# Per-token factors turned once and broadcast from DRAM, and the queries' factor moved into the exponential

## The chip, the cores and the metric

The kernel runs on one core of one Trainium2 chip. Its time is the device time of one execution in microseconds (us). The core has TensorE (PE; its weight loads are listed apart as PEld), VectorE (DVE), ScalarE (ACT), GpSimd (POOL), and SyncE (SP), which in this kernel issues every DMA, in order. TensorE writes its results to PSUM, eight banks of 128 partitions x 512 float32; the other tiles lie in SBUF.

## The reference

One decoder layer on 1024 tokens of width 1024, in float32. Each norm multiplies a token by a factor of its own, and the change is about those factors and about the one of the mLSTM heads:

```python
def rmsnorm(x, g):
    y = xf * lax.rsqrt(jnp.mean(xf * xf, axis=-1, keepdims=True) + EPS)
    return (y * g).astype(x.dtype)

h = rmsnorm(x, ln1[l]);  z = h @ w_in[l]
...                                    # 4 mLSTM heads (dh 128), 8 forgetting-attention heads (dh 64)
mh = mlstm_chunkwise(mq, mk, mv, ig, lf)
mh = mh * lax.rsqrt(jnp.mean(mh * mh, axis=-1, keepdims=True) + EPS)
mh = mh * ml_norm[l]
ml_out = mh * sigmoid(ml_o)
x = x + concatenate([ml_out, fx_out]) @ w_out[l]
x = x + cross_attention(rmsnorm(x, ln_x[l]), rmsnorm(mem, ln_mem[l]), w_xq[l], w_xkv[l], w_xo[l])
u = relu(rmsnorm(x, ln2[l]) @ w_ff1[l]);  x = x + (u * u) @ w_ff2[l]
return rmsnorm(x, ln_f)

def cross_attention(h, memn, w_q, w_kv, w_o):          # 4 heads of 256, 256 memory tokens
    q = h @ w_q
    ...
    s = einsum('bqhd,bmhd->bhqm', q, k) * (X_DH ** -0.5)
    p = softmax(s, axis=-1)
    ...
```

## The kernel before

**Layout and precision.** Activations lie feature-major: 128 features on the partitions, tokens along the free axis, in two halves of 512 tokens (`hf` 0 and 1). A product is made of three matmuls (`mm3`, L184 to L186) of a high and a low part of each operand; `split` (L129) cuts a tile in two: ScalarE writes the high part (L132, with a scale L135), VectorE the low part (L133, with a scale L136). A weight tile is loaded to `wr` (L172, two buffers), cut to `wh` and `wl` (three buffers each), and used for 24 matmuls of 512 columns for each half.

**A factor per token.** A norm's factor is made token-major: sums of squares by matmuls against a column of ones (L233, L216), then `rsqrt_cols` (L192), small VectorE steps around one power on GpSimd (L202), give a column tile [128 tokens, n blocks] such as `rcol` or `fac`. Feature-major data need it along the free axis, the same on all partitions. `spread` (L209) does that: for each block of 128 tokens one float32 matmul of the column, broadcast over 128 columns as weights, against the identity; the result is a PSUM bank, read from there or copied by ScalarE to the constant tile `row` [128, 1024] (`row_m` for the memory tokens).

**Where factors are spread.** (1) The first norm: half 0 inside the hand-ordered first stage (L391 to L394), half 1 in `spread_second` (L407), called between two token blocks of `token_major`. Readers: every projection of the mLSTM and the forgetting heads (L489, L618, L643). (2) The memory norm in `mem_prepare` (L283). (3) Each mLSTM head: at the end of `ml_head` (L601 to L610) the factor `fac` is spread half by half; two VectorE multiplies, a split and two stores to `mix` follow. (4) The cross-attention norm, after each half of the mixer's second projection (L1042); the readers are the queries (L1052) and `xo_sink` (L1199). (5) The final factor `inv`, at job 30 of the first MLP product (L1390 to L1394); `stretch` (L1370) then rescales the residual with it, tile by tile through DRAM. (6) `finish` (L1482), the last norm.

**The mLSTM loop.** `ml_project(hd)` (L631) makes a head's projections: keys with a convolution (`conv_silu`), the forgetting heads' queries (`fx_project(0)`), the carried state, queries, forgetting keys, output gate. `ml_head(hd)` (L551) does the head's attention: it loads the decay row `nmb` by a broadcast from the DRAM tile `rows` into the buffer "a" (L558), exponentials of it on ScalarE (L569), a mask on GpSimd (L571), the multiply with the scores on VectorE (L572). Program order is `ml_head(0)`, `ml_project(1)`, `ml_head(1)` and so on.

**Order.** Except for stages in `in_order()`, which chains the instructions of each compute engine in the order written (the first stage, and every `slot` of the forgetting attention, L938), a planner sets each engine's order and the order of SP's issues: it runs through the program with a model of the durations and takes, in program order of preference, what is ready. On the chip each engine then keeps that order. Tiles are taken by tag from rotating buffers (`BUFS`, L70: "a" and "y" one, the others two); a tile waits until the one before it in its buffer has been read or stored.

**Cross attention.** `cross_head` (L1046), one for each head and half: two products of 24 matmuls into the banks `mm` and `m2`; for each, VectorE multiplies by 1/16 and by `row` into `qf` (L1052) and `qf` is split; then scores, maximum (L1070), exponential (L1072), reciprocal, transposes (L1080), values.

## Time and profile before

Three runs took 1584.74, 1588.86 and 1590.78 us (median 1588.86). The profiled execution took 1586.37 us; its span, from the first to the last instruction, is 1584.7 us, at a mean granted TensorE clock of 0.991.

| stage | stretch (us) | TensorE busy (us) | VectorE busy (us) | DMA share |
|---|---|---|---|---|
| first norm, first values | 0 to 40 | 32.70 | 29.30 | 0.59 |
| mLSTM values, gates, first head | 40 to 180 | 137.75 | 88.93 | 0.27 |
| mLSTM heads | 180 to 330 | 150.00 | 101.36 | 0.31 |
| last head, fox values | 330 to 440 | 106.44 | 62.13 | 0.58 |
| forgetting attention | 440 to 640 | 192.62 | 145.70 | 0.73 |
| mixer's projection | 640 to 700 | 55.90 | 45.73 | 0.82 |
| cross heads | 700 to 850 | 150.00 | 80.20 | 0.38 |
| cross output, begin of MLP | 850 to 960 | 109.26 | 93.11 | 0.46 |
| first MLP product | 960 to 1200 | 232.22 | 197.24 | 0.76 |
| second MLP product | 1200 to 1540 | 338.98 | 239.22 | 0.66 |
| last norm and output | 1540 to 1585 | 28.50 | 25.08 | 0.29 |

In the profile's lines a group is named by its line in the kernel, its engine, its operation and the tiles it writes and reads ("sc<-ident,c_fac": a PSUM tile of the tag sc from the identity and the column tile fac). In the timeline the columns are start, duration, engine (SPq: SP's queue, the issue of a DMA), line, operation, tiles, and in brackets the idle time of the engine before it and what ended it. A wait is written "who waits <- for whom: us in total, times, longest".

### The profile page before, as it was taken

The page shows a single profiled execution, that of the slowest core. Times are in us where ns is not written, and L with a number is a line of the kernel's source. Part 1 is how long each engine was busy: PE and PEld are TensorE (multiplying, and loading weights), DVE is VectorE, ACT ScalarE, POOL GpSimd, SP SyncE. Part 2 cuts the span into 40 slices and gives each one's busy share as a digit, 9 for nine tenths or more (in the row PEclk, how much of TensorE's full clock was granted, in tenths as well). Part 3 has the DMA queues.
Part 4 walks back from the last instruction along what each step waited for, and adds up shares of the span by engine and source line. Part 5 has one row for each costly group of instructions (what it writes and reads, how often), then busy time and mean ns, then how long its engine had stood idle before and what let it go on. Part 6 is the DMA issues. An engine that isn't in the chain of part 4 may idle for free.

```text
span 1584.7 us, 22226 instructions
## 1 busy us (share of the span) xinstructions
PE 1534.4 (97%) x7836; PEld 1280.1 (81%) x7836; DVE 1108.0 (70%) x1752; ACT 724.1 (46%) x1323; POOL 440.3 (28%) x476
## 2 busy tenths in 40 slices
PE   8999999999999999999999999999999999999995
PEld 8888888889887887778888877777778778888885
DVE  7656666665677785765457887888877877766775
ACT  7324343333577673544344466666665422111153
POOL 0003030413344431421100022433343543333314
PEclk9999999999999999999999999999999999999998
DMA  5322222435686857853344438777877966656632
GB/s 209 112 73 91 100 87 90 126 107 162 214 238 194 262 211 263 297 198 122 120 140 154 163 123 294 243 270 272 279 259 280 380 262 239 239 239 239 253 133 107
DMA packets 123271, 310.72 MB, mean 196 GB/s; under 512 B 13764, under 2 KB 28228, under 8 KB 115224
## 3 DMA queue, kind: packets, MB, share of 16 engines
q1 hardware_dynamic: 123160, 309.31, 56.2%
q8 instruction: 61, 1.00, 0.3%
q14 instruction: 50, 0.41, 0.1%
HBM read 205.24 MB, written 104.02 MB: 195 GB/s over the span
## 4 chain that ended last, share of the span: by engine, by line
PE 46%; DVE 8%; DMA 7%; ACT 3%; issue 3%; POOL 1%; SPq 0%; DVEq 0%; ACTq 0%; POOLq 0%
PE sc L184 4%; PE sc L186 4%; PE sc L185 4%; PE tp L184 3%; PE tp L186 3%; PE tp L185 3%; PE m L184 3%; PE mm L184 3%; PE mm L186 3%; PE mm L185 3%; PE m L186 3%; PE m L185 3%; PE ov L184 2%; PE ov L185 2%; PE ov L186 2%
## 5 line engine op out<-in xcount | busy, mean ns | idle before, releaser
L132 ACT ACTIVATE wh<-wr 128x1024 fp32r<-128x1024 f32 (+2 forms) x105 | 105.4, 1005 | 136.6 <-PE mm L186 35.2
L184 PE MATMUL tp<-act,wl 128*128 128x512 f32 (+1 forms) x388 | 152.4, 393 | 1.4 <-ACT row L1287 0.7
L185 PE MATMUL tp<-act,wh 128*128 128x512 f32 (+1 forms) x388 | 151.8, 391 | 0.0
L186 PE MATMUL tp<-act,wh 128*128 128x512 f32 (+1 forms) x388 | 151.6, 391 | 0.0
L133 DVE TENSOR_TENSOR wl<-wr,wh 128x1024 fp32r<-128x1024 f32 (+2 forms) x105 | 127.2, 1213 | 21.3 <-ACT wh L132 20.9
L184 PE MATMUL m<-act,wl 128*128 128x512 f32 (+1 forms) x348 | 135.2, 389 | 1.0 <-DVE wl L133 0.6
L186 PE MATMUL m<-act,wh 128*128 128x512 f32 (+1 forms) x348 | 133.4, 383 | 0.0
L185 PE MATMUL m<-act,wh 128*128 128x512 f32 (+1 forms) x348 | 133.3, 383 | 0.0
L184 PE MATMUL mm<-act,wl 128*128 128x512 f32 (+1 forms) x308 | 119.9, 389 | 2.9 <-DVE wl L133 1.3
L185 PE MATMUL mm<-act,wh 128*128 128x512 f32 (+1 forms) x308 | 118.3, 384 | 0.0
L186 PE MATMUL mm<-act,wh 128*128 128x512 f32 (+1 forms) x308 | 118.3, 384 | 0.0
L184 PE MATMUL sc<-act,wl 128*128 128x512 f32 (+1 forms) x296 | 114.9, 389 | 2.8 <-DVE wl L133 2.2
L185 PE MATMUL sc<-act,wh 128*128 128x512 f32 (+1 forms) x296 | 114.1, 386 | 0.0
L186 PE MATMUL sc<-act,wh 128*128 128x512 f32 (+1 forms) x296 | 113.5, 385 | 0.0
L1358 POOL TENSOR_TENSOR z<-wr 128x256 f32<-128x256 f32 x56 | 50.5, 922 | 168.1 <-DMA wr<-w_ff2q 132.1
L132 ACT ACTIVATE w<-wr 128x768 fp32r<-128x768 f32 (+1 forms) x30 | 24.5, 818 | 153.7 <-PE sc L186 82.9
L184 PEld LDWEIGHTS tp<-act,wl 128*128 128x128 f32 x388 | 72.9, 188 | 18.8 <-DVE wl L133 1.5
L186 PEld LDWEIGHTS tp<-act,wh 128*128 128x128 f32 x388 | 72.9, 188 | 16.2
L185 PEld LDWEIGHTS tp<-act,wh 128*128 128x128 f32 x388 | 72.9, 188 | 15.9
L132 ACT ACTIVATE wh<-z 128x1024 fp32r<-128x1024 f32 (+1 forms) x54 | 55.5, 1028 | 59.6 <-POOL z L1358 26.9
L184 PEld LDWEIGHTS m<-act,wl 128*128 128x128 f32 x348 | 65.6, 189 | 15.1 <-DVE wl L133 1.0
L186 PEld LDWEIGHTS m<-act,wh 128*128 128x128 f32 x348 | 65.4, 188 | 13.3
(657 smaller groups left out, 4288.2 us busy)
## 6 DMA issues: line engine op xcount, KB each, us to landing
act<-right SPq DMA_DIRECT2D x49, 1024.0 KB
right<-w SPq DMA_DIRECT2D x56, 256.0 KB
wr<-w_ff2q SPq DMA_DIRECT2D x28, 512.0 KB
wr<-w_ff SPq DMA_DIRECT2D x25, 512.0 KB
right<-r_d SPq DMA_DIRECT2D x49, 256.0 KB
right<-r_e SPq DMA_DIRECT2D x49, 256.0 KB
act<-fqk SPq DMA_DIRECT2D x48, 256.0 KB
wr<-w_in SPq DMA_DIRECT2D x20, 512.0 KB
```

Source lines behind the costliest of these rows:

```text
L132: s.activation(hi, src, AF.Copy)
L133: return v.tensor_tensor(out=lo, in0=src, in1=hi.bitcast(F32), op=ALU.subtract)
L184: nc.tensor.matmul(ps, w[1], x[0], start=first, stop=False, skip_group_check=more)
L185: nc.tensor.matmul(ps, w[0], x[1], start=False, stop=False, skip_group_check=more)
L186: nc.tensor.matmul(ps, w[0], x[0], start=False, stop=last, skip_group_check=more)
L1358: g.tensor_tensor(out=o, in0=x, in1=y, op=op)
```

## The change

A new helper `to_row` turns a column tile of n blocks into n rows by one TensorE transpose, copies the small result to SBUF on ScalarE, stores it in a DRAM tile, and loads it back with a broadcast over all 128 partitions. It takes the place of `spread` in the cases (1) to (5); `finish` keeps it. Besides that:

- The first norm's two halves are laid out together, between token blocks 1 and 2 of `token_major` (`row_first`).
- In `ml_head` the part from the spread on becomes three later steps of a generator: it stops after `fac`, and `ml_project` of the next head continues it after its key projection (transpose, store, load of half 0), after `fx_project(0)` (multiplies, split, stores of half 0; load of half 1) and after `carried` (the same of half 1). For the last head the steps come after the slots 2, 6 and 10 that lead the forgetting attention in. The rows are loaded into the buffer "a"; the fox values (`fv_sink`) rotate through "b", "p", "c" in place of "b", "a", "c".
- The cross norm of half 0 is worked out after the third output tile of half 1 of the mixer's projection, that of half 1 after the first cross head.
- The queries are no longer multiplied by the norm's factor: PSUM is split at once with the scale 1/16, and the factor enters the exponential as its scale per partition (there tokens lie on the partitions, so `rcol` serves as it is); the maxima are multiplied by it.
- The final factor of both halves is laid out at job 30 at once.

```diff
+    rowd = dram.tile([4, T], F32, name="rowd")
+
+    def to_row(dst, cols, n, at, bank=None):
+
+        ps = (bank or ov_)()
+        nc.tensor.transpose(ps[:n, :P], cols, ident)
+        s.activation(dst[:n, :P], ps[:n, :P], AF.Copy)
+        load(at.rearrange("o (t q) -> (o t) q", t=n), dst[:n, :P])
+        w = min(dst.shape[1], n * P)
+        return load(dst, at[:, :w].broadcast_to([P, w]))
...
-        s.activation(row_m, rsqrt_row(acc, rcol_m, 2, 2), AF.Copy)
+        rsqrt_sums(acc, rcol_m, 2, 2)
+        to_row(row_m, rcol_m, 2, rowd[1:2, :NM])
...
-                ps = ov_()
-                spread(ps, rcol[:, 0:4], 4)
-                s.activation(row[:, 0:TH], ps, AF.Copy)
...
-    def spread_second():
-        ps = ov_()
-        spread(ps, rcol[:, 4:8], 4)
-        s.activation(row[:, TH:], ps, AF.Copy)
+    def row_first():
+        to_row(row, rcol, 8, rowd[0:1])
...
+    facd = dram.tile([MLH, T], F32, name="facd")
...
         v.tensor_tensor(out=fac, in0=fac, in1=rd, op=ALU.mult)
+        yield
         for hf in range(2):
-            fb = sc()
-            spread(fb, fac[:, 4 * hf : 4 * hf + 4], 4)
+            fb = w2("a")
+            at = facd[hd : hd + 1]
+            if hf == 0:
+                to_row(fb, fac, 8, at, sc)
+            else:
+                load(fb, at[:, TH:].broadcast_to([P, TH]))
+            yield
             y = nums[hf]
...
-        o = rotate("b", "a", "c").bitcast(F32R).rearrange("p (h e c) -> p h e c", h=4, e=2)
+        o = rotate("b", "p", "c").bitcast(F32R).rearrange("p (h e c) -> p h e c", h=4, e=2)
...
+    closing = iter(())
...
         yk = conv_silu(MLH + hd, *k)
+        next(closing, None)
         fx_project(0, hd)
+        next(closing, None)
         state = carried(hd, yk)
+        next(closing, None)
         yq = conv_silu(hd, *q)
...
-    token_major(a["w_mv"], mv_sink, (1,), {2: spread_second, 4: gate_rows})
+    token_major(a["w_mv"], mv_sink, (1,), {2: row_first, 4: gate_rows})
...
-        ml_head(hd, *ready)
+        closing = ml_head(hd, *ready)
+        next(closing)
...
-    for _ in range(LEAD_):
+    for i in range(LEAD_):
         slot(False, 0)
+        if i in (2, 6, 10):
+            next(closing, None)
...
             split(hi[:, n], lo[:, n], t, vec[:, VEC["ln_x"] + n :][:, 0:1])
             square_sum(acc, t, n == 0, add=g)
             if hf == 1 and n == KT - 3:
                 mix_done.append(done)
+            if hf and n == 2:
+                row_second(0, acc0)
+
+        def row_second(hf, acc):
+            c = rcol[:, 4 * hf : 4 * hf + 4]
+            rsqrt_sums(acc, c, 4)
+            at = slice(hf * TH, hf * TH + TH)
+            to_row(row[:, at], c, 4, rowd[2:3, at])
 
         out_proj(a["w_out_b"], mix_fx[hf], hf, full_sink)
-        s.activation(row[:, hf * TH : hf * TH + TH], rsqrt_row(acc, rcol[:, 4 * hf : 4 * hf + 4], 4), AF.Copy)
         h2.append((hi, lo))
+        acc0 = acc
...
-                qf = w2("f")
-                v.scalar_tensor_tensor(out=qf, in0=ps, scalar=1.0 / 16.0, in1=row[:, hf * TH : hf * TH + TH], op0=ALU.mult, op1=ALU.mult)
-                split(*t, qf)
+                split(*t, ps, 1.0 / 16.0)
...
                 v.tensor_reduce(out=mxc[:, i - 1 : i + 1], in_=sp, axis=mybir.AxisListType.X, op=ALU.max, negate=True)
+
+                v.tensor_tensor(out=mxc[:, i - 1 : i + 1], in0=mxc[:, i - 1 : i + 1], in1=rcol[:, 4 * hf + i - 1 : 4 * hf + i + 1], op=ALU.mult)
         for i in range(4):
-            s.activation(pr[:, i], sps[i // 2][:, i % 2], AF.Exp, bias=mxc[:, i : i + 1], accum_out=den[:, i : i + 1])
+            s.activation(pr[:, i], sps[i // 2][:, i % 2], AF.Exp, bias=mxc[:, i : i + 1], scale=rcol[:, 4 * hf + i : 4 * hf + i + 1], accum_out=den[:, i : i + 1])
...
             for _ in steps:
                 pass
+            if hd == hf == 0:
+                row_second(1, acc0)
...
-            for hf in range(2):
-                ps = bank()
-                spread(ps, inv[:, 4 * hf : 4 * hf + 4], 4)
-                s.activation(row[:, hf * TH : hf * TH + TH], ps, AF.Copy)
+            to_row(row, inv, 8, rowd[3:4], bank)
```

More of the change, by code (lines that the diff above doesn't have):

```diff
@@ L1035, in full_sink @@
                     mix_fx.append(mix_load(MLH + KX, KT, 1))
+            split(hi[:, n], lo[:, n], t, vec[:, VEC["ln_x"] + n :][:, 0:1])
+            square_sum(acc, t, n == 0, add=g)
             if hf == 1 and n == KT - 3:
                 mix_done.append(done)
-            split(hi[:, n], lo[:, n], t, vec[:, VEC["ln_x"] + n :][:, 0:1])
-            square_sum(acc, t, n == 0, add=g)
+            if hf and n == 2:
[5 more added lines that the diff above has]
+            to_row(row[:, at], c, 4, rowd[2:3, at])
         out_proj(a["w_out_b"], mix_fx[hf], hf, full_sink)
-        s.activation(row[:, hf * TH : hf * TH + TH], rsqrt_row(acc, rcol[:, 4 * hf : 4 * hf + 4], 4), AF.Copy)
         h2.append((hi, lo))
+        acc0 = acc
     def cross_head(hd, hf, oh, ol):
```

## The prediction

> **What bounds the kernel now.** I read the page first, then the busy time by stretches, then TensorE's own waits.
>
> ```profile
> PE 1534.4 (97%) x7836; PEld 1280.1 (81%) x7836; DVE 1108.0 (70%) x1752; ACT 724.1 (46%) x1323; POOL 440.3 (28%) x476
> ...
> 180.00:250.00 70.00, 70.00 (x348) 58.67 (x348) 43.65 (x72) 25.67 (x43) 15.47 (x18) 1.00 0.27 93
> 250.00:330.00 80.00, 80.00 (x402) 67.18 (x401) 57.71 (x88) 29.20 (x46) 19.24 (x21) 1.00 0.35 113
> 440.00:640.00 200.00, 192.62 (x1174) 163.22 (x1174) 145.70 (x345) 128.77 (x325) 71.38 (x106) 0.99 0.73 234
> 640.00:700.00 60.00, 55.90 (x264) 44.88 (x263) 45.73 (x58) 31.45 (x52) 23.86 (x16) 1.00 0.82 284
> 700.00:760.00 60.00, 60.00 (x314) 50.60 (x313) 31.27 (x45) 24.88 (x53) 9.69 (x16) 1.00 0.35 116
> 760.00:850.00 90.00, 90.00 (x450) 75.15 (x449) 48.93 (x72) 37.96 (x77) 7.36 (x16) 1.00 0.40 136
> 960.00:1200.00 240.00, 232.22 (x986) 184.26 (x986) 197.24 (x233) 148.04 (x231) 91.03 (x61) 0.99 0.76 263
> ```
>
> Each stretch lists its length and the busy time of PE, PEld, DVE, ACT, POOL, then the granted clock, the DMA share and GB/s. TensorE has no idle time in the mLSTM heads (180 to 330) or in the cross heads (700 to 850), 4.1 us around the end of the mixer's projection (640 to 700) and 7.8 us in the first MLP product (960 to 1200). So the kernel is bound by TensorE. An instruction taken off TensorE is worth its own time; what is taken off VectorE is worth nothing while TensorE stays full; and what is put on the DMA queue costs only where TensorE ends up waiting for it. TensorE's waits that touch the change are two, and the second has its cause one row further back, on ScalarE:
>
> ```profile
> PE ov L212 <- DVE rcol L207: 2.4, 1, 2.4
> PE sc L216 <- ACT r_c L583: 1.4, 1, 1.4
> ...
> 375.17 0.47 ACT L135 ACTIVATE r_a<-mm,rcol 128x256 fp32r<-128x256 f32 x1 [7.43 <-DMA fvd<-r_a]
> ```
>
> The first is the cross-norm's spread, which sits in TensorE's order before its factor is ready. The second waits for a square that stands on ScalarE behind a cut of the fox values (L628), which waited 7.43 us for the one buffer "a" to be stored.
>
> **Removed from TensorE.** The spreads (L212) are plain float32 matmuls, two instructions for a column:
>
> ```profile
> L212 PE MATMUL sc<-ident,c_fac x64: 270/275/275, 178.7 to 389.0; 128*128 128x128 f32 x64
> L212 PE MATMUL ov<-ident,rcol x32: 270/275/347, 31.4 to 694.5; 128*128 128x128 f32 x32
> L212 PE MATMUL mm<-ident,gcol x8: 270/275/275, 964.5 to 965.3; 128*128 128x128 f32 x8
> L212 PE MATMUL tp<-ident,gcol x8: 270/275/275, 985.9 to 986.6; 128*128 128x128 f32 x8
> L212 PE MATMUL ov<-ident,rcol_m x4: 273/275/276, 87.4 to 87.8; 128*128 128x128 f32 x4
> ...
> 178.47 0.39 PE L184 MATMUL tp<-act,wl 128*128 128x512 f32 x1
> 178.69 1.95 PE L212 MATMUL sc<-ident,c_fac 128*128 128x128 f32 x16
> 180.40 0.48 PE L185 MATMUL tp<-act,wh 128*128 128x512 f32 x1
> 180.72 0.40 PE L186 MATMUL tp<-act,wh 128*128 128x512 f32 x1
> ```
>
> All of these go (c_fac 64, rcol 32, gcol 16, rcol_m 4: 116 instructions); those of `finish` stay. Durations overlap, so I price by starts. Ordinary 512-column matmuls start 0.22 to 0.23 us apart (178.47 to 178.69). Between 178.47 and 180.72 there are two such steps, 0.46 us, and the sixteen spreads: 2.25 - 0.46 = 1.79 us, 0.112 us each, the slower first start behind them (0.32 us) included. 116 x 0.112 = 13.0 us.
>
> **Added to TensorE.** Nine transposes: mem 1, `row` at the start 1, heads 4, cross norm 2, final factor 1.
>
> ```profile
> L1080 PE MATMUL tp<-ident,z x64: 270/272/273, 705.4 to 830.8; 128*128 128x128 f32 x64
> ...
> 705.17 0.39 PE L185 MATMUL mm<-act,wh 128*128 128x512 f32 x1
> 705.40 1.04 PE L1080 MATMUL tp<-ident,z 128*128 128x128 f32 x8
> 706.19 0.36 PE L184 MATMUL sc<-w,r_c 128*128 128x256 f32 x1
> 706.39 0.28 PE L185 MATMUL sc<-w,r_b 128*128 128x256 f32 x1
> ```
>
> L1080 transposes 8 blocks in each of 8 heads, 64 in all, so a transpose is one instruction. Eight take 705.40 to 706.19, 0.10 each, and the next start comes about 0.08 late: 0.18 for one that stands alone. 9 x 0.18 = 1.6 us. Net: 13.0 - 1.6 = 11.4 us off TensorE.
>
> **The way through DRAM.** Each turned row costs a ScalarE copy, a store, and a broadcast load (a second one in each head), all on SP's queue: 9 stores and 13 loads, 22 issues. A full-width copy out of PSUM is the upper bound for the narrow copy; the price of the trip stands where the kernel already does it with the gates' `rows`:
>
> ```profile
> L410 ACT ACTIVATE row<-ov x1: 597/597/597, 55.3 to 55.3; 128x512 f32<-128x512 f32 x1
> ...
> 70.94 0.24 SPq L455 DMA_DIRECT2D rows<-w  x1
> 73.15 0.34 SPq L505 DMA_DIRECT2D c_m<-rows  x1
> 73.47 0.67 DVE L489 TENSOR_TENSOR z<-tp,row 128x512 f32<-128x512 f32 x1
> ...
> 171.83 0.32 SPq L540 DMA_DIRECT2D r_c<-rows  x1
> 174.98 0.72 ACT L541 ACTIVATE r_c<-r_c,c_m 128x512 f32<-128x512 f32 x1 [1.21 <-DMA r_c<-rows]
> ```
>
> From the store's issue to the issue of a load that reads it 2.21 us; from a 128x512 broadcast load to its reader, which was waiting, 3.15 us. A trip is 0.60 + 2.21 + 3.15 = 6.0 us where one spread and copy took some 1.5. For the full-width `row` (twice the bytes) I take up to 3.15 more, 9.1 us. At the start: `row` was complete at 55.9 and first read at 73.47, 17.6 us of cover; without it VectorE would hold the first convolution's two banks by what is over. At the final factor the first reader stood here:
>
> ```profile
> 982.47 0.69 DVE L1378 TENSOR_TENSOR r_e<-r_e,row 128x512 f32<-128x512 f32 x1 [2.04 <-DMA r_e<-x2d]
> 988.67 0.58 ACT L1394 ACTIVATE row<-tp 128x512 f32<-128x512 f32 x1
> ```
>
> The spread of the first half ran at 964.5, 18 us ahead of 982.47, again more than 9.1. Its second half was only copied at 988.67; one transpose needs both halves of `row` free, and if that sets its start, the rescalings slip some 15 us. They hold only a rotating buffer, so I take nothing, with 2.4 (the longest wait above) as the dear end. The mem row is read only by the key units of the fox stage; nothing waits. The cross rows are now read only by the sinks after all cross heads; nothing waits.
>
> **Heads.** The factor's second half of the work (two multiplies, split, store) now stands between pieces of the next head's projections, and its rows go through the single buffer "a", which the next head's decay row (L558) needs too.
>
> ```profile
> 173.84 0.17 DVE L600 TENSOR_TENSOR c_fac<-c_fac,c_rd 128x8 f32<-128x8 f32 x1
> 201.50 0.69 DVE L572 SCALAR_TENSOR_TENSOR r_b<-sc,r_b 128x512 f32<-128x512 f32 x1
> L605 DVE SCALAR_TENSOR_TENSOR r_f<-r_f,vec,sc x8: 741/744/748, 179.8 to 389.8; 128x512 f32<-128x512 f32 x8
> SPq L172 <- DVE wl L133: 208.3, 44, 14.2
> ```
>
> The factor is ready at 174.0. New chain: 0.2 transpose + 0.6 copy + 2.2 + 3.15 + 0.74 multiply, then the second half 3.15 + 0.74, then the next decay row 3.15: 187.9. Head 1 first multiplies by its weights at 201.5, after an exponential and a masking (about 1.5), so 12 us are left. Cover: the projections that fill TensorE meanwhile. Cost nothing; without that slack, its overrun at each head (the slower rival).
>
> **Queries.** L1052, 16 of it, goes; the split reads PSUM itself, its second step as a scalar_tensor_tensor with one PSUM operand (the row of L605, 0.74) in place of 0.69; 16 two-column multiplies of about 0.17 (L600) come in ahead of the exponentials.
>
> ```profile
> L1052 DVE SCALAR_TENSOR_TENSOR r_f<-m,row 128x512 f32<-128x512 f32 x8 | 5.5, 689 | 19.3 <-PE m L186 19.3
> ACT z L1072 <- DVE c_mx L1070: 17.5, 10, 4.6
> ```
>
> VectorE saves 16 x (0.69 - 0.17 - 0.06), 7 us, all beside a full TensorE: worth nothing. The bank was free 0.69 after its last matmul; now it is held through a ScalarE step (0.6, as L410) and 0.74, and ScalarE can stand up to 4.6 us waiting for a maximum: 5.9 at most, against the 24 x 0.23 = 5.5 us of the other bank's product. So 0 to 16 x 0.4 = 6 us; I take 0, since the mean of that wait is 1.75.
>
> **Stalls.** The fox values rotate through "p" (two buffers) instead of "a": the 1.4 us should go (0 to 1.4; I take 1.4). The cross-norm's stall of 2.4: its chain of small VectorE steps is not shortened, only placed elsewhere, and there are two transposes that may meet it: from -2.4 to +2.4, I take 0.
>
> **Sum.** The profiled execution took 1586.4 us (span 1584.7 and 1.7 around it): 1586.4 - 11.4 - 1.4 = 1573.6. It lies 2.5 under the median of the three runs, so on the median's scale 1576. About 0.5% (7.9 us) is what the measurement tells from no change.
>
> **Rivals.**
> *Most of it was idle anyway.* For: the cross and final spreads (32 instructions, 3.6 us) lie in the stretches where TensorE has idle time, and both cross transposes could meet a late factor, one stall of 2.4 more. Against: the heads alone are 64 of the 116 and have no idle time. 11.4 - 3.6 - 2.4 = 5.4 saved: 1583.5.
> *The heads' chain through "a" (slower).* SP issues in order; behind a weight load that waits for its buffer a factor's load waits too. Those waits are 208.3/44 = 4.7 on the mean, 14.2 at most. Three loads a head: two mean waits and one longest are 23.6, less 12 of slack: 11.6 at each of the three heads that have a successor, 35 us, less 12.8: 1611. It decides from 12 + 12.8/3 = 16 us of added wait a head, three mean waits and a bit. Against: the buffer is late only if the planner puts the issues in that order, and it did not for `rows`. The Trainium skill speaks for it: by DMA: Bandwidth & Descriptors (Anatomy of one DMA) most of a DMA's fixed time of about 2 us is the wait for the write's receipt, so turning two instructions into a store and a dependent load buys latency for a few hundred bytes. By that rule alone the trip's first leg is about 2 us; the 2.21 above agrees. A second rule, of SBUF — State Buffer (Who interferes with whom), lets a VectorE instruction with two SBUF inputs block against a GpSimd one that reads SBUF; the factor multiply becomes one. By it, were each of the two multiplies held once for as long as it takes (0.74), the slack would be 10.5 and this rival decide from 14.8; no row here has this multiply in that state.
> *More than the sum.* Both stalls go and the planner fills better: 1586.4 - 11.4 - 2.4 - 1.4 = 1571.2, on the median's scale 1574, and up to 4 less if a few of the 7.8 idle us of the MLP go with the freed banks: 1570.
>
> **Numbers.** Forecast 0.60 (its own range 1571 to 1583: the stall's ±2.4 and the bank's 6), idle anyway 0.16, slower 0.17, more 0.07. Range 1569 to 1594: it leaves out most of the slower case. Faster (under 1581.0): 0.55 + 0.07 + 0.03 of the idle case = 0.65; same 0.05 + 0.13 = 0.18; slower 0.17.
>
> **What would show it.** L212 down to the 16 instructions of `finish`; nine transposes of about 0.3 us; TensorE's busy time down by about 11; the stretch 180 to 330 still without idle time and the fourth head's factor earlier by about 6 us. Wrong if TensorE waits appear before L184 with a decay weight or a factor row behind them, if VectorE stands at the multiply for a DMA long enough to hold banks, or if the order of unrelated work changes and brings idle time of its own.

## The result, and the profile after

| | median us | lowest to highest | runs | profiled execution | its span |
|---|---|---|---|---|---|
| before | 1587.76 | 1584.74 to 1590.78 | 4 | 1586.37 | 1584.7 |
| after | 1575.11 | 1572.11 to 1577.46 | 4 | 1577.46 | 1575.7 |

The ratio after to before is 0.9919, with a 95% interval of 0.9893 to 0.9946: 12.7 us less by the medians, and at least 0.5%. The profiled execution of after is the slowest of its four, so its span shows only 9.0 of them. In what follows "after" is the changed kernel, and line numbers are its own (or those of the experiment in question): `to_row` is L248 (transpose), L250 (store) and L252 (load), the heads' second load L616, their multiply L619, the decay row's load L566.

First TensorE's busy time on the page of after, then the stretches (length; busy time of PE, PEld, DVE, ACT, POOL; granted clock, DMA share, GB/s):

```profile
PE 1520.8 (97%) x7729; PEld 1264.3 (80%) x7729; DVE 1104.8 (70%) x1752; ACT 722.6 (46%) x1325; POOL 440.2 (28%) x476
```

```profile
180.00:330.00 150.00, 150.00 (x729) 124.93 (x729) 102.26 (x158) 54.62 (x92) 33.55 (x39) 1.00 0.36 112
330.00:440.00 110.00, 106.16 (x781) 97.74 (x781) 68.18 (x161) 58.01 (x140) 36.20 (x50) 1.00 0.68 202
...
640.00:700.00 60.00, 56.36 (x252) 44.77 (x251) 44.06 (x52) 31.01 (x51) 24.19 (x18) 0.97 0.77 267
700.00:850.00 150.00, 150.00 (x765) 125.56 (x764) 78.19 (x123) 64.69 (x131) 19.16 (x29) 1.00 0.41 134
...
960.00:1200.00 240.00, 230.94 (x973) 182.99 (x972) 200.31 (x232) 147.19 (x230) 89.94 (x61) 0.99 0.75 259
```

TensorE's busy time fell by 1534.4 - 1520.8 = 13.6 us, with 7836 - 7729 = 107 instructions fewer, as 116 spreads less nine transposes should give. What lies in the span outside it grew from 50.3 (1584.7 - 1534.4) to 54.9 us, so 4.6 were given back as idle time. The mLSTM heads (180 to 330) and the cross heads (700 to 850) still have no idle time: the heads' longer chain through DRAM did not reach TensorE.

The groups of spreads and transposes in after (count; shortest, median, longest in ns; first and last start):

```profile
L212 PE MATMUL ov<-ident,c_r x8: 270/275/275, 1545.6 to 1546.4; 128*128 128x128 f32 x8
L212 PE MATMUL mm<-ident,c_r x8: 275/398/554, 1562.4 to 1568.8; 128*128 128x128 f32 x8
L248 PE MATMUL sc<-ident,c_fac x4: 270/270/270, 179.7 to 381.6; 128*8 128x128 f32 x4
L248 PE MATMUL ov<-ident,rcol x3: 269/270/273, 52.1 to 728.9; 128*4 128x128 f32 x2, 128*8 128x128 f32 x1
L248 PE MATMUL ov<-ident,rcol_m x1: 276/276/276, 92.6 to 92.6; 128*2 128x128 f32 x1
L248 PE MATMUL mm<-ident,gcol x1: 270/270/270, 959.4 to 959.4; 128*8 128x128 f32 x1
```

The sixteen spreads of `finish` are left, and nine transposes stand in place of 116 spreads. TensorE's new or remaining waits around the change:

```profile
PE sc L184 <- ACT r_p L1319: 4.6, 2, 4.4
...
PE ov L248 <- DVE rcol L207: 2.4, 1, 2.4
```

and, of the waits between 50 and 80 us alone, where before has none:

```profile
PE m L184 <- DVE wl L133: 1.2, 1, 1.2
PE tp L184 <- DVE act L136: 1.1, 1, 1.1
```

The wait for the square (1.4, L216) is gone. The cross-norm's 2.4 is the same wait, now of a transpose instead of a spread. New are the 4.4 in the first MLP product and the 1.2 and 1.1 at the start. Then the chain through DRAM, from the timeline of SP's queue (first head, then final factor) and of VectorE (first head):

```profile
180.33 0.28 SPq L250 DMA_DIRECT2D facd<-r_a  x1
183.53 0.33 SPq L252 DMA_DIRECT2D r_a<-facd  x1
187.68 0.32 SPq L616 DMA_DIRECT2D r_a<-facd  x1
...
191.89 0.32 SPq L566 DMA_DIRECT2D r_a<-rows  x1
...
961.35 0.31 SPq L250 DMA_DIRECT2D rowd<-row  x1
...
966.11 0.41 SPq L252 DMA_DIRECT2D row<-rowd  x1
```

```profile
186.90 0.75 DVE L619 SCALAR_TENSOR_TENSOR r_f<-r_f,vec,r_a 128x512 f32<-128x512 f32 x1 [2.42 <-DMA r_a<-facd]
...
191.10 0.75 DVE L619 SCALAR_TENSOR_TENSOR r_f<-r_f,vec,r_a 128x512 f32<-128x512 f32 x1 [0.99 <-DMA r_a<-facd]
```

VectorE does stand for the row (2.42 and 0.99 us here), and the next decay row's load goes out at 191.89. The prediction had that row complete at 187.9; with its 3.15 us to land it is there at 195.0, so 7 of the 12 us of slack are used and about 5 are left. Most of the 7 is one step: the factor was ready at 175.0 (1.1 later than before), but its transpose started only at 179.7, 4.7 us behind it. TensorE notices nothing.

### The profile page after: what moved, and what is told of

It is laid out like the page before. It is cut to its first block, busy times and chain, and to the rows that moved or that the text cites. A ratio compares the mean times of both kernels' runs of the same rounds, so it can differ in the third digit from the quotient of the medians.

```text
span 1575.7 us, 22034 instructions
## 1 busy us (share of the span) xinstructions
PE 1520.8 (97%) x7729; PEld 1264.3 (80%) x7729; DVE 1104.8 (70%) x1752; ACT 722.6 (46%) x1325; POOL 440.2 (28%) x476
## 4 chain that ended last, share of the span: by engine, by line
PE 46%; DVE 9%; DMA 7%; ACT 3%; issue 2%; POOL 1%; SPq 0%; DVEq 0%; ACTq 0%; POOLq 0%
PE sc L184 4%; PE sc L185 4%; PE sc L186 4%; PE tp L184 4%; PE tp L185 3%; PE tp L186 3%; PE m L184 3%; PE m L186 3%; PE m L185 3%; PE mm L184 3%; PE mm L186 3%; PE mm L185 3%; DVE w L133 2%; DVE wl L133 2%; PE ov L184 1%
## 5 line engine op out<-in xcount | busy, mean ns | idle before, releaser
L184 PE MATMUL tp<-act,wl 128*128 128x512 f32 (+1 forms) x456 | 179.3, 393 | 4.8 <-DVE wl L133 2.9
L185 PE MATMUL tp<-act,wh 128*128 128x512 f32 (+1 forms) x456 | 178.4, 391 | 0.0
L186 PE MATMUL tp<-act,wh 128*128 128x512 f32 (+1 forms) x456 | 177.5, 390 | 0.0
L186 PE MATMUL mm<-act,wh 128*128 128x512 f32 (+1 forms) x336 | 129.0, 384 | 0.0
L185 PE MATMUL mm<-act,wh 128*128 128x512 f32 (+1 forms) x336 | 128.8, 383 | 0.0
L185 PE MATMUL m<-act,wh 128*128 128x512 f32 (+1 forms) x316 | 121.9, 386 | 0.0
L186 PE MATMUL m<-act,wh 128*128 128x512 f32 (+1 forms) x316 | 121.7, 385 | 0.0
L184 PE MATMUL sc<-act,wl 128*128 128x512 f32 (+1 forms) x260 | 101.9, 392 | 7.7 <-ACT r_p L1319 4.6
L184 PEld LDWEIGHTS tp<-act,wl 128*128 128x128 f32 x456 | 85.7, 188 | 25.8 <-DVE wl L133 4.7
L186 PEld LDWEIGHTS tp<-act,wh 128*128 128x128 f32 x456 | 85.7, 188 | 19.2
L186 PE MATMUL sc<-act,wh 128*128 128x512 f32 (+1 forms) x260 | 101.1, 389 | 0.0
L185 PE MATMUL sc<-act,wh 128*128 128x512 f32 (+1 forms) x260 | 101.1, 389 | 0.0
L185 PEld LDWEIGHTS tp<-act,wh 128*128 128x128 f32 x456 | 85.8, 188 | 19.0
L184 PEld LDWEIGHTS mm<-act,wl 128*128 128x128 f32 x336 | 63.3, 188 | 16.8 <-DVE wl L133 1.8
L186 PEld LDWEIGHTS mm<-act,wh 128*128 128x128 f32 x336 | 63.2, 188 | 12.8
```

The costliest lines, as they stand in the source:

```text
L184: nc.tensor.matmul(ps, w[1], x[0], start=first, stop=False, skip_group_check=more)
L185: nc.tensor.matmul(ps, w[0], x[1], start=False, stop=False, skip_group_check=more)
L186: nc.tensor.matmul(ps, w[0], x[0], start=False, stop=last, skip_group_check=more)
```

## The experiments

Twelve kernels, each timed in rounds with the kernel before on the same chip. All ratios are to the kernel before of the same rounds; the medians of before were 1586.4 to 1586.9 us. "Against after" compares two such ratios. The interval of after alone is about 4 us to either side, so a difference to it of less than 4 or 5 us can't be told from none.

| kernel | median us | ratio | 95% interval |
|---|---|---|---|
| heads_alone | 1579.75 | 0.9949 | 0.9935 to 0.9963 |
| queries_alone | 1585.74 | 0.9989 | 0.9979 to 0.9998 |
| rows_alone | 1593.39 | 1.0038 | 1.0024 to 1.0052 |
| rows_queries | 1582.32 | 0.9977 | 0.9964 to 0.9991 |
| spreads_too | 1582.38 | 0.9966 | 0.9951 to 0.9981 |
| fv_a | 1586.85 | 0.9999 | 0.9986 to 1.0012 |
| at_once | 1573.65 | 0.9918 | 0.9900 to 0.9935 |
| trips_2 | 1577.39 | 0.9933 | 0.9917 to 0.9948 |
| trips_5 | 1622.15 | 1.0211 | 1.0193 to 1.0228 |
| first_spread | 1573.22 | 0.9912 | 0.9897 to 0.9928 |
| last_spread | 1576.53 | 0.9936 | 0.9920 to 0.9952 |
| both_spreads | 1580.91 | 0.9953 | 0.9935 to 0.9970 |

**Is it TensorE's own time?** The theory of the prediction is that a spread is worth 0.112 us wherever TensorE is full. `spreads_too` is after, with the heads' 64 spreads run as well into banks that nobody reads.

```diff
             if hf == 0:
+                for e in range(2):
+                    spread(sc(), fac[:, 4 * e : 4 * e + 4], 4)
                 to_row(fb, fac, 8, at, sc)
```

> The changed kernel with the heads' 64 spread instructions run as well, their result unread. Theory, the gain is TensorE's own time: 64 x 0.112 = 7.2 us over the changed kernel, that is 5 to 6 under the kernel before. Rival, the gain comes from waits that the heads no longer make (the spread's place in the order, buffer a, a PSUM bank): 0 to 2 us over the changed kernel.

It lost 7.5 us against after (0.9966 - 0.9919 = 0.47% of 1587), and the intervals don't overlap. With both intervals taken together the loss lies between about 2.6 and 12.3 us: the rival's 0 to 2 are out, the size is known only roughly. The same from the other side, `heads_alone`: the kernel before with only the heads' part of the change, the rotation of the fox values included.

```diff
+        yield
         for hf in range(2):
-            fb = sc()
-            spread(fb, fac[:, 4 * hf : 4 * hf + 4], 4)
+            fb = w2("a")
+            at = facd[hd : hd + 1]
+            if hf == 0:
+                to_row(fb, fac, 8, at, sc)
+            else:
+                load(fb, at[:, TH:].broadcast_to([P, TH]))
+            yield
...
-        o = rotate("b", "a", "c").bitcast(F32R).rearrange("p (h e c) -> p h e c", h=4, e=2)
+        o = rotate("b", "p", "c").bitcast(F32R).rearrange("p (h e c) -> p h e c", h=4, e=2)
...
```

> The kernel before with the heads' part alone (64 spread instructions go, 4 transposes come, the fox values rotate through p). Theory, TensorE's own time: 64 x 0.112 - 4 x 0.18 = 6.4 us, and 1.4 of the wait at the fox values: 7.8 us under the kernel before. Rival, the way through DRAM is on the path (the chain through buffer a): not faster than before, by up to 35 us slower.

It gained 8.1 us (0.51%; 5.9 to 10.3 by the interval), where 7.8 were expected. The place can be read from one row in each trace: the multiply that makes a head's factor, its first and last start among the four heads. Before, after, heads alone, and after with the spreads run again, in this order:

```profile
L600 DVE TENSOR_TENSOR c_fac<-c_fac,c_rd x4: 166/166/168, 173.8 to 385.4; 128x8 f32<-128x8 f32 x4
```

```profile
L608 DVE TENSOR_TENSOR c_fac<-c_fac,c_rd x4: 167/168/169, 174.9 to 379.6; 128x8 f32<-128x8 f32 x4
```

```profile
L612 DVE TENSOR_TENSOR c_fac<-c_fac,c_rd x4: 166/167/168, 173.3 to 378.0; 128x8 f32<-128x8 f32 x4
```

```profile
L608 DVE TENSOR_TENSOR c_fac<-c_fac,c_rd x4: 159/168/168, 173.9 to 384.4; 128x8 f32<-128x8 f32 x4
```

From the first to the fourth head it is 211.6 us before, 204.7 after, 204.7 with the heads alone and 210.5 with the spreads back. Three heads lie between: 6.9 us gained, of which 5.8 come back with the spreads, 1.9 a head against 16 x 0.112 = 1.8. What is left, 1.1, is near the stall of 1.4 less three transposes. No run has the new rotation without the rows in "a", so the stall's own 1.4 is read from the trace only.

**What are the queries and the rows worth?** `queries_alone` is the kernel before with these lines:

```diff
-                qf = w2("f")
-                v.scalar_tensor_tensor(out=qf, in0=ps, scalar=1.0 / 16.0, in1=row[:, hf * TH : hf * TH + TH], op0=ALU.mult, op1=ALU.mult)
-                split(*t, qf)
+                split(*t, ps, 1.0 / 16.0)
...
+                v.tensor_tensor(out=mxc[:, i - 1 : i + 1], in0=mxc[:, i - 1 : i + 1], in1=rcol[:, 4 * hf + i - 1 : 4 * hf + i + 1], op=ALU.mult)
...
-            s.activation(pr[:, i], sps[i // 2][:, i % 2], AF.Exp, bias=mxc[:, i : i + 1], accum_out=den[:, i : i + 1])
+            s.activation(pr[:, i], sps[i // 2][:, i % 2], AF.Exp, bias=mxc[:, i : i + 1], scale=rcol[:, 4 * hf + i : 4 * hf + i + 1], accum_out=den[:, i : i + 1])
```

`rows_alone` is the kernel before with the first, mem, cross and final rows through DRAM, of which these two hunks stand for all; the queries still read the cross row. `rows_queries` has both parts and not the heads'.

```diff
-        s.activation(row_m, rsqrt_row(acc, rcol_m, 2, 2), AF.Copy)
+        rsqrt_sums(acc, rcol_m, 2, 2)
+        to_row(row_m, rcol_m, 2, rowd[1:2, :NM])
...
-            for hf in range(2):
-                ps = bank()
-                spread(ps, inv[:, 4 * hf : 4 * hf + 4], 4)
-                s.activation(row[:, hf * TH : hf * TH + TH], ps, AF.Copy)
+            to_row(row, inv, 8, rowd[3:4], bank)
```

> The kernel before with the queries' part alone. Theory: VectorE's 7 us lie beside a full TensorE, so 0 against the kernel before. Rival 1, VectorE's time counts: 7 us faster. Rival 2, the banks mm and m2 are held too long: up to 6 us slower.

> The kernel before with the rows of the norms and of the final factor alone (52 spread instructions go, 5 transposes come), queries and heads as before. Theory: 52 x 0.112 - 5 x 0.18 = 4.9 us faster. Rival, the part in stretches with idle TensorE is worth nothing: 3.6 less, 1.3 us faster. Since the changed kernel's trace has its start 1.2 us late and not 1.6 us early, some 3 us of the 4.9 may be missing here too.

> The kernel before with the rows and the queries, heads as before. rows_alone was 6 us slower: its TensorE stood 6.86 us in the first cross heads for the queries, which waited for the row's way through DRAM. Theory, the queries' edit takes that row off the path and is worth nothing else: the stall is gone and the run is 3 to 5 us faster than before. Rival, the rows lose their time elsewhere too (start, final factor): still 2 us or more slower than before.

The queries alone gained 1.7 us (0.11%), little more than the 0 they were priced at. The rows alone were to gain and lost 6.0 us (0.38%), a miss. With the queries' part beside them they gain 3.6 (0.23%), within the 3 to 5 expected; this and the heads' 8.1 make 11.7 of the 12.7. TensorE's wait and the rows that explain it, in `rows_alone` (a wait, then the timeline, then three stretches):

```profile
PE mm L184 <- DVE r_f L1067: 6.9, 1, 6.9
```

```profile
681.98 0.29 SPq L250 DMA_DIRECT2D rowd<-row  x1
...
688.07 0.32 SPq L252 DMA_DIRECT2D row<-rowd  x1
...
691.84 0.79 PE L184 MATMUL mm<-act,wl 128*128 128x512 f32 x1 [6.86 <-DVE r_f L1067]
```

```profile
676.00:685.00 9.00, 6.81 (x29) 5.19 (x29) 8.10 (x9) 4.66 (x7) 4.29 (x3) 1.00 0.98 364
...
692.00:697.00 5.00, 5.00 (x12) 3.94 (x13) 1.68 (x3) 1.05 (x2) 0.00 (x0) 0.50 0.21 84
697.00:702.00 5.00, 5.00 (x31) 4.46 (x31) 0.69 (x1) 0.09 (x1) 0.00 (x0) 0.91 0.01 3
```

L1067 there is the multiply of the queries by the cross row, which the queries' part removes. The row's load goes out 6.09 us behind its store, at a time when the DMA engines are full (share 0.98, 364 GB/s); the multiply waits for it, the product's bank stays full, and TensorE stands 6.86 us. Then it runs at half clock for 5 us (0.50). So the two parts are not a sum. The row through DRAM is harmless only because the queries' factor has moved into the exponential, where it is read from the column.

**Is the buffer of the fox values more than its stall?** `fv_a` is after with the old rotation.

```diff
-        o = rotate("b", "p", "c").bitcast(F32R).rearrange("p (h e c) -> p h e c", h=4, e=2)
+        o = rotate("b", "a", "c").bitcast(F32R).rearrange("p (h e c) -> p h e c", h=4, e=2)
```

> The changed kernel with the fox values rotating through b, a, c as before. Theory: TensorE's wait of 1.4 us behind a cut that waits for buffer a to be stored comes back, and the last head's rows take the same buffer: 1.4 to 3 us slower than the changed kernel. Rival, that wait was harmless: within 1 us.

It lost 12.7 us against after (0.9999 - 0.9919 = 0.80%; 8 to 17 by the intervals), the whole gain of the change, where 1.4 to 3 were expected. Waits, a stretch and ScalarE's row, from its trace:

```profile
PE sc L714 <- ACT act L726: 7.7, 6, 3.0
PE tp L184 <- DVE r_a L136: 3.0, 1, 3.0
```

```profile
330.00:440.00 110.00, 98.07 (x680) 88.95 (x680) 59.52 (x137) 48.06 (x115) 30.15 (x41) 0.94 0.57 171
...
380.00:390.00 10.00, 3.66 (x13) 1.91 (x12) 6.62 (x19) 4.39 (x13) 1.49 (x2) 0.70 0.39 132
```

```profile
388.27 0.47 ACT L135 ACTIVATE r_a<-tp,rcol 128x256 fp32r<-128x256 f32 x1 [2.14 <-DVE r_f L619]
```

With the change, "a" carries the last head's factor rows. TensorE is busy for 3.66 of 10 us there, and two of its waits make up most of the rest. Before the one of 2.47 us, a cut of the fox values that also wants "a" stands on ScalarE until the multiply L619 has read the rows, and the exponentials behind it are late. Before the one of 3.02 us, VectorE itself stands at L619 for a row (1.33 us), with small steps of the fox scores behind it. In the whole stretch TensorE is idle 8.1 us more than in after (98.07 against 106.16), and works at a granted clock of 0.94 where after has 1.00. The new rotation is not a small gain beside the rest; it is what makes the heads' way through "a" affordable. The one line also moved the planner's order (the fourth head's factor starts at 374.3, in after at 379.6), and how the 12.7 us divide among these waits was not tested.

**Does the heads' chain have slack, and does the slower rival exist?** Extra trips lengthen the chain without any other work: the first half of the row is stored and loaded again, once (`trips_2`, with range(1)) or four times (`trips_5`).

```diff
+    facd2 = dram.tile([4, MLH, TH], F32, name="facd2")
...
                 to_row(fb, fac, 8, at, sc)
+                for e in range(4):
+                    load(facd2[e, hd : hd + 1], fb[0:1, 0:TH])
+                    load(fb, facd2[e, hd : hd + 1].broadcast_to([P, TH]))
```

> The changed kernel with one more store and broadcast load of half 0's row in each head, 5.4 us more in the chain through buffer a, of 12 us of slack. Theory: no difference to the changed kernel (within 1 us). Rival, the chain is on the path: 3 x 5.4 = 16 us slower.

> The changed kernel with four more trips in each head, 21 us more in the chain, over the slack of 12 us by 9. Prediction's price: 3 heads x 9 = 28 us slower. Rival, the planner finds other work for TensorE (the next projections, the fox values) and the overrun costs less than 5 us in all.

One more trip costs nothing that can be told from after (0.9933 against 0.9919, with overlapping intervals), as the 5 us left of the slack allow: in the first head the extra trip takes 4.3 us (the row's load goes out at 182.21, its repeat at 186.50). Four more cost 46 us (1.0211 - 0.9919 = 2.92%) where 28 were expected, a miss. Waits, then the multiply that makes a head's factor, then two stretches, of the latter:

```profile
PE sc L718 <- ACT act L730: 20.8, 12, 15.5
PE tp L184 <- DVE r_f L552: 10.7, 1, 10.7
...
PE tp L184 <- DVE w L666: 6.7, 1, 6.7
```

```profile
L609 DVE TENSOR_TENSOR c_fac<-c_fac,c_rd x4: 166/167/169, 173.7 to 414.8; 128x8 f32<-128x8 f32 x4
```

```profile
180.00:330.00 150.00, 139.26 (x639) 114.57 (x638) 90.30 (x132) 49.41 (x82) 30.05 (x38) 0.94 0.37 118
330.00:440.00 110.00, 97.09 (x656) 87.98 (x655) 54.67 (x121) 39.59 (x89) 23.99 (x29) 0.94 0.49 149
```

The mechanism of the slower rival is real: past the slack, TensorE waits 6.7, then 10.7, then 15.5 us, the last in the fox scores, after the two stretches shown. From the first to the fourth factor it is 241.1 us against 204.7 in after, 12.1 a head. The four trips take 18.5 us in the first head (182.13 to 200.60), so some 6 us of them were covered: near the 5 us that were left, and not the 12 that the expectation still counted with. The other 10 us come behind the fourth factor. The stalls also cost clock (0.94 over both stretches), which the 46 us contain and the expectation did not.

**Does the deferral matter?** `at_once` writes the head's last part in one piece, not between pieces of the next head's projections.

```diff
-        closing = ml_head(hd, *ready)
-        next(closing)
+        for _ in ml_head(hd, *ready):
+            pass
```

> The changed kernel with each head's last part written at once behind its factor, through DRAM as now, not between the next head's projections. Theory, the planner takes what is ready, so the place in the program is only a preference: within 2 us of the changed kernel. Rival, the later place is what hides the way through DRAM: each head pays the trip, 4 x 6.0 = 24 us slower.

It is the same as after (0.9918). The rival's 24 us are out, and no effect of the order in which the pieces are written can be told.

**Would some spreads be better left?** At the start, after shows the two waits of 1.2 and 1.1 us, behind the final factor the 4.4. `first_spread` and `last_spread` put the old spreads back at one of these places, `both_spreads` at both.

```diff
+                ps = ov_()
+                spread(ps, rcol[:, 0:4], 4)
+                s.activation(row[:, 0:TH], ps, AF.Copy)
...
-    def row_first():
-        to_row(row, rcol, 8, rowd[0:1])
+    def spread_second():
+        ps = ov_()
+        spread(ps, rcol[:, 4:8], 4)
+        s.activation(row[:, TH:], ps, AF.Copy)
...
-            to_row(row, inv, 8, rowd[3:4], bank)
+            for hf in range(2):
+                ps = bank()
+                spread(ps, inv[:, 4 * hf : 4 * hf + 4], 4)
+                s.activation(row[:, hf * TH : hf * TH + TH], ps, AF.Copy)
```

> The changed kernel with the first norm spread as before (16 spread instructions back, one transpose less: 1.6 us more of TensorE). In the changed kernel's trace the first convolution's product is read 1.2 us later than before although TensorE had less to do. Theory, the new order around the row's way loses about 3 us there: 1 to 2 us faster than the changed kernel. Rival, TensorE's own time decides here as in the heads: 1.6 us slower.

> The changed kernel with the final factor spread as before (16 spread instructions back, one transpose less: 1.6 us more of TensorE). Theory, the 4.37 us wait of TensorE at 1005 in the changed kernel's trace (2.48 and 0.49 at 993 and 997 in the one before) comes from the rescalings' shifted order, so this gains 1.4 and loses 1.6: no difference above 1 us. Rival, the row's way is harmless: 1.6 us slower.

> The changed kernel with the first norm and the final factor both spread as before, that is heads, memory and cross norm by the new way. From first_spread (two waits of 1.1 and 1.2 us gone against 1.6 us of TensorE) and last_spread (4.35 us of wait for 1.95, against 1.6): 1 to 2 us faster than the changed kernel; TensorE's time alone would make it 3.2 slower.

`first_spread` is the lowest measured, 0.9912, but its interval covers the 0.9919 of after: not told apart. `last_spread` is 0.17% above after, with overlapping intervals. The waits of its trace between 960 and 1060 us:

```profile
PE sc L184 <- DVE wl L133: 2.0, 1, 2.0
PE sc L184 <- DVE w L1306: 1.9, 1, 1.9
```

The 4.4 is gone and 3.9 stand there. So the row through DRAM does cause that wait, and the spreads that avoid it (16 x 0.112 less a transpose, 1.6 us) gain nothing over it. `both_spreads` was to be 1 to 2 us faster than after and was 5.4 slower by the ratios (0.9953 - 0.9919 = 0.34%), a miss; its interval overlaps that of after by a little and that of `first_spread` not at all. Its spreads' own time is 32 x 0.112 - 2 x 0.18 = 3.2 us. The rest is not settled; a part of it stands in these stretches of its trace:

```profile
400.00:405.00 5.00, 3.03 (x27) 2.79 (x26) 1.18 (x5) 1.61 (x4) 0.65 (x1) 1.00 1.11 361
405.00:410.00 5.00, 4.30 (x17) 2.98 (x18) 3.52 (x10) 3.36 (x11) 1.79 (x4) 0.53 1.04 302
410.00:415.00 5.00, 5.00 (x33) 4.61 (x32) 2.76 (x8) 2.97 (x8) 1.68 (x6) 0.79 0.86 253
```

After has nearly the same two idle gaps there (1.87 and 0.70 us against 1.97 and 0.70) but keeps the full clock (330 to 440 above, 1.00); here the granted clock falls to 0.53 and 0.79, which takes 5 x 0.47 + 5 x 0.21 = 3.4 us (the last section has more on it).

## Why the prediction was right, and where it was not

- **TensorE's own time, 11.4 us: right.** Its busy time fell by 13.6, and the fourth head's factor starts 5.8 us earlier (379.6 against 385.4), where about 6 were forecast. The price of a spread was tested directly: 64 of them cost 7.5 us where 7.2 were expected. A transpose was cheaper than its 0.18: the one at 179.73 makes the second matmul behind it start at 180.07 where 179.96 would follow without it, 0.11 us, which is 0.6 less for the nine. The rest of the 2.2 between 11.4 and 13.6 is not accounted for.
- **The stall at L216, 1.4 us: right as a stall, mis-sized as an edit.** It is gone, but the new rotation also keeps the fox values out of the way of the factor rows, and without it 12.7 us are lost (`fv_a`). The prediction costed the edit by the wait that it removes and not by the one that the rest of the change would have made.
- **Queries, 0: right alone, incomplete.** 1.7 us by themselves, so the bank held through ScalarE cost nothing that shows. But "The cross rows are now read only by the sinks after all cross heads; nothing waits" is worth as much as the rows' loss without it: -3.6 against +6.0 us. The cover of the cross row is this edit, and the prediction named it without pricing what happens when it is gone.
- **The trip through DRAM, 2.21 us from store to load: one value for something that varies.** The nine trips of after took 1.20 to 5.47 us (median 3.16), and the cross row's in the rows alone 6.09; the last section has them beside the DMA share. The price was taken from one place, with a share of 0.47 between the two issues. The Trainium skill's page DMA: Bandwidth & Descriptors (Anatomy of one DMA) puts the fixed part of a DMA at about 2 us, in a section on DMAs that GpSimd issues; here SyncE issues them, and the trips lie on both sides of that figure. A head's store is 4 KB, not the few hundred bytes that the prediction names.
- **The heads' slack, 12 us: right that it holds, mis-sized.** The chain came out 7 us longer. The prediction put 0.2 us for the transpose right behind the factor at 174.0; but TensorE's order has it 4.7 us behind, and the old spread stood there just the same (178.69, a line that the prediction shows). The later factor is 1.1 of the 7, the longer trip 1.0. What was left was enough for after and for one more trip (`trips_2`), and the size showed in `trips_5`.
- **The start: missed.** Sixteen spreads less a transpose, 1.6 us, were to be gained ahead of the first convolution. It came 1.2 us later instead, against 73.47 before:

```profile
74.70 0.67 DVE L496 TENSOR_TENSOR z<-tp,row 128x512 f32<-128x512 f32 x1
```

  VectorE did not wait for the row there, so the 17.6 us of cover held. The delay comes through the gate rows. TensorE transposes them 2.36 us later than before (61.27 against 58.91), since the first convolution's matmuls now stand ahead of them and themselves wait 1.1 us; VectorE's chain on these rows starts 2.36 us later too (63.00 against 60.64), and the convolution's product is read behind it. That product is now read ahead of a weight cut and not behind it, which gives 1.1 us back. The waits of 1.2 and 1.1 us stand in all nine traces with the first row through DRAM and in none of the five without it (before, `heads_alone`, `queries_alone`, `first_spread`, `both_spreads`). So they come with that row; by what step the planner then chose this order is not shown.
- **The final factor, 0 with 2.4 as the dear end: at the dear end.** In the first MLP product 4.4 us of one wait stand where before had this one:

```profile
PE sc L184 <- DVE w L1274: 2.5, 1, 2.5
```

  With the smaller waits between 960 and 1060 us it is 5.7 against 3.7, 2.0 more. Ten us ahead of it ScalarE, in after, waited for the store of a rescaled tile:

```profile
995.43 0.63 ACT L132 ACTIVATE r_d<-w 128x512 fp32r<-128x512 f32 x1 [4.40 <-DMA x2d<-r_d]
```

  The step "they hold only a rotating buffer, so I take nothing" failed there: the buffer "d" in which the rescaled tile waits for its store is wanted by a cut on ScalarE, and what stands behind the cut is late. The chain from the one row to the other is argued, not tested; that the row through DRAM brings the wait is shown by `last_spread`.
- **The cross-norm's stall, 0: right as a wait, incomplete.** It is 2.4 before and after. In the trace of after the clock drops behind it and in that of before it does not (last section), 1.7 us for which the sum has no term.
- **The sum** was within 1 us of the median, and that closeness is in part luck: the misses cancel, more off TensorE than priced against idle time of 4.6 that was not, and after itself is known only to about 4 us. The forecast's own range is not what its two terms give: 1576 with -2.4 to +2.4 and 0 to 6 is 1574 to 1584, not 1571 to 1583.
- **The rivals.** *Idle anyway* (1583.5) is out: the upper end of the interval is 0.9946 x 1587.76 = 1579.2. *The heads' chain* (1611) did not happen, since the slack held; its mechanism exists: 46 us in `trips_5`. The rule of the Trainium skill named beside it (SBUF — State Buffer, Who interferes with whom), VectorE blocked by GpSimd, was not put to the test. In the trace of after no GpSimd instruction lies beside any of the eight multiplies, and all took 0.75 us, close to the 0.74 that they took with one operand in PSUM.

```profile
L619 DVE SCALAR_TENSOR_TENSOR r_f<-r_f,vec,r_a x8: 750/752/753, 186.9 to 395.0; 128x512 f32<-128x512 f32 x8
```

  *More than the sum* (1574) can't be told from the forecast by its time, but its reasons are wrong: of its stalls one stayed, and the MLP gained idle time instead of losing some.

## What to carry to other kernels

Where TensorE is full, count its instructions and price them by their starts: the term that was tested alone came out at 7.5 us (2.6 to 12.3) for 7.2 expected, while VectorE's 7 us saved with the queries gave 1.7. When small broadcasts move from a full engine to a way through DRAM, ask of each one who reads it first and how long after; here the heads had slack for one more trip, and the cross row had none until its reader was moved. Measure the parts of such a change alone and together before dropping one as worthless: the queries' edit and the buffer's rotation looked like 0 and 1.4 us, and the rest needs both of them.

## What the runs showed of the hardware

**The same stall can cost once or nearly twice.** The cross-norm's wait is 2.36 us long in after and in `first_spread`. The stretches of 3 us from its begin, first after, then `first_spread` (granted clock third from the end):

```profile
672.00:675.00 3.00, 0.64 (x4) 0.45 (x4) 3.00 (x6) 1.30 (x3) 1.04 (x1) 1.00 0.88 269
675.00:678.00 3.00, 3.00 (x11) 2.33 (x10) 2.73 (x3) 2.76 (x5) 2.57 (x2) 0.63 1.03 392
678.00:681.00 3.00, 3.00 (x12) 2.43 (x11) 3.00 (x3) 1.06 (x1) 1.02 (x1) 0.80 1.03 408
```

```profile
666.00:669.00 3.00, 0.64 (x5) 0.23 (x3) 3.00 (x6) 0.92 (x2) 1.42 (x1) 1.00 0.86 279
669.00:672.00 3.00, 3.00 (x14) 2.44 (x14) 2.73 (x3) 2.98 (x6) 2.17 (x2) 1.00 1.02 369
```

In after the clock then drops, 3 x 0.37 + 3 x 0.20 = 1.7 us of it, which is half the clock for 3.4 us (it is 0.50 from 676 to 679); in `first_spread` it does not. `rows_alone` with its longer stall left out, twelve traces have this wait (2.0 to 2.4 us) between 640 and 700 us: seven of them show a clock of 0.96 from 660 to 700, after among them, and five have 1.00, before among them. The 1.2 us wait at the start divides the nine traces that have it in the same way: from 70 to 80 us the clock is 0.83 in after and in `rows_queries`, 1.7 us lost, and 1.00 in the other seven. The Trainium skill's page TensorE: Matmul & The Clock Gate (Part 1: The HAM clock gate) states two clocks, full and half, and a free-running window of about 3.4 us: the half clock, the 3.4 us and the dependence on the moment agree. It puts the drop behind an idle window of that length; here stalls of 1.2 and 2.4 us were enough. So a TensorE stall of 1.2 to 2.4 us has a price of itself or of itself and 1.7 us (3.4 behind the two stalls of `both_spreads` above), and a change elsewhere that shifts it can turn one into the other. It varies between executions of one kernel too: the six of `both_spreads` go from 1576.73 us at a mean clock of 0.992 to 1583.39 at 0.989, and 0.003 of 1580 is 4.7 of these 6.7 us. Differences of a few us between kernels, `both_spreads` and after among them, can be of this kind; that they are was not shown.

**A trip through DRAM took 1.1 to 6.8 us from store to load, and its length goes with the DMA share.** The nine trips of after, with the DMA share between the two issues:

| row | store issued | store to load (us) | DMA share | other issues between |
|---|---|---|---|---|
| memory norm | 93.22 | 1.20 | 0.00 | 1 |
| first norm | 52.97 | 1.23 | 0.01 | 0 |
| second head | 250.31 | 1.23 | 0.01 | 0 |
| cross norm, half 1 | 729.45 | 2.13 | 0.44 | 0 |
| third head | 320.99 | 3.16 | 0.56 | 0 |
| first head | 180.33 | 3.20 | 0.53 | 0 |
| fourth head | 383.13 | 4.29 | 0.79 | 1 |
| final factor | 961.35 | 4.76 | 0.31 | 2 |
| cross norm, half 0 | 678.34 | 5.47 | 1.02 | 1 |

The first and the third head's store went out 0.7 us behind a weight load of 512 KB, the second head's did not. The other eleven kernels that have such rows give the same picture. Of 90 trips in all, 31 with a share of up to 0.16 took 1.1 to 1.6 us, 29 with 0.42 to 0.61 took 1.7 to 3.3, nine with 0.74 to 0.94 took 2.7 to 5.2, and twelve with 0.97 or more took 3.9 to 6.8. The final factor's nine are the exception, 4.7 to 5.9 us at 0.31 to 0.37, each with two other stores issued in between. No run changed the share or the queue alone, so that the one or the other makes the trip longer is not shown.
